# A hybrid encoder trunk in split fp32: the mixer's output projection as seven half-size products, and four MLP blocks begun with half the tokens

## The chip, the cores and the metric

The kernel runs on one core of one Trainium2 chip. The metric is the device time of one execution in microseconds (us), lower is better. The kernel before was run three times: 1082.97, 1083.27 and 1083.28 us, median 1083.27 us. The engines are named as in the profile: PE is TensorE, DVE VectorE, ACT ScalarE, POOL GpSimd, SP the queue that issues the transfers.

## The reference

One layer over 512 tokens of width 1024. What matters here is the end of the token mixing and the MLP:

```python
g = sigmoid(gates + b_gate)
g_ssd, g_attn = g[..., :D_MODEL], g[..., D_MODEL:]
mixed = (g_ssd * y_ssd + g_attn * y_attn) @ w_o          # 512x1024 @ 1024x1024
x = x + rmsnorm(mixed, post_mix_norm)
h = rmsnorm(x, pre_mlp_norm)
f = square(relu(h @ w_mlp_in)) @ w_mlp_out               # width 4096
x = x + rmsnorm(f, post_mlp_norm)
```

`y_ssd` is itself a product with `w_ssd_out` (2048 x 1024). Everything ahead of it (input projection, state-space scan, windowed attention) is the same in both kernels.

## The kernel before

**Products.** Every fp32 operand is split into two parts, `hi` (rounded by a cast on ACT) and `lo` (the rest, a subtract on POOL or DVE), and a product is three matmuls, hi x hi, hi x lo and lo x hi, into one PSUM bank (`mm3`, L436; the matmul is at L430, transposes at L434). A matmul multiplies one 128x128 tile against 512 columns, or 256.

**Order.** The program is a list of quanta (`build`, L1633). Each has weight chunks that are loaded (`wr`, three buffers), split into `wh` and `wl` (three buffers) ahead of time, and a function that issues its matmuls. The program written so is then put in order by a planner (`Planner`, `chain`, L529), which simulates it with costs and due times and fixes one static order of instructions for each engine. An engine works strictly in that order: an instruction that waits holds up all behind it. The order of the SP queue, which issues the loads, is fixed in the same way.

**Buffers.** PSUM has eight banks of 128x512: a ring of three called `pp` and a ring of five called `ps` (`bank`, L395). Other tiles of 128x512 come from 83 SBUF slots (`slots.get`, `slots.put`), handed out again first in, first out.

**The stages around the change**, in order:
- `ssd_out` (`ssd_out_quanta`, L1303): eight blocks of 128 output features, all 512 tokens, 16 k-tiles x 3 = 48 matmuls each. The first two blocks do 14 k-tiles first, and their last two k-tiles come later (`rest`), because the last two tiles of `y` wait for an rstd that passes through small DMAs (`yT` L1235, `yl` L1283). After each block `ssd_out_done` (L1287) applies the gates: two DVE operations into the gate's own SBUF slot (L1290, L1291), then a split with scale 0.5 into `mh` and `ml` (L450, L451), features on the partitions.
- `w_o`: 16 tiles of 128x512, loaded by `load_wo`, split by `split_wo`: cast on ACT (L447), subtract on DVE (L448).
- The mixer (`mix_quantum`, L1354): for each of four token tiles, two halves of 512 output columns, 8 k-tiles x 3 = 24 matmuls each, 192 in all. Then Square with a row sum on ACT (L1369), three 128x1 steps on POOL ending in a `pow` (L421 to L425), the norm, the residual `x1`, a second Square and `pow`, and the scaled rows `h2` (L1374 to L1379).
- `flip_h2` (L1390): 16 PE transposes for each half of the tokens put `h2` with features on the partitions, and ACT and DVE split it (L455, L456). The first is placed before the mixer's last token tile, the second after the first of the MLP's halves.
- `up_halves` (L1465): the first SPL = 3 blocks of the first MLP product are begun with tokens 0 to 255 (24 matmuls of 256 columns each) while the rest is normed and flipped, and finished with tokens 256 to 511. Further blocks take all 512 columns (`up_quantum`). After a pair of blocks, `up_done` and `combine` (L1428) make the operands A11, A12, A22 and S1 to S4 of the second product.
- The second MLP product (`folded_quanta`, L1492) is computed in four parts, each as one 2x2 block product with seven half-size products in place of eight: operands A and S from `combine`, weights B11, B21, B22 and T1 to T4, where T1 to T4 are sums of weight tiles made on DVE (L1510 to L1521). A half-size product is 2 token tiles x 4 k-tiles x 3 = 24 matmuls of 512 columns. Its sums are gathered into `acc` (L1598 copy on ACT, L1601 add on DVE). Part 3 takes the order A11, A12, S2, S1, S4, S3, A22.

The small 128x1 steps of the last norm stand at L1617 and L1619, its multiply by the gain at L1623, its residual update at L1629, its `pow` at L1626.

Of the kernel before, what the change touches and what calls it, by code (L numbers as in the profile page):

```python
# [29 lines left out]
LAST_LO = dict(LO, **{n: [LO[n][0], [(0, 512)]] for n in ('T1', 'T2', 'T3', 'T4')})  # L30

# [337 lines left out]
class Trunk:  # L369
# [917 lines left out]
    def ssd_out_done(self, ps, m):  # L1287
        nc = self.nc
        t = self.gate[m]
        nc.vector.scalar_tensor_tensor(t, t, 1.0, ps, op0=ALU.add, op1=ALU.mult)  # L1290
# [3 lines left out]
        self.slots.put(t, self.gate[8 + m])  # L1294
        self.mix.append((hi, lo))
        if m == 7:
            for a in self.ys:
                self.slots.put(*a)
            for k in range(0, 8, 2):
                self.split_wo(1, k)  # L1300
            self.load_x()

    def ssd_out_quanta(self):  # L1303

        w = self.d_w_ssd_out_b
        banks = []

        def most(parts):
            ps = self.bank("pp")
            banks.append(ps)  # L1310
            for k in range(14):
                wh, wl = parts[k // 8]
# [10 lines left out]
        tail = w[0:2, 1, :, 6:8].rearrange("m p k n -> p m (k n)")  # L1323
        return [Quantum([(w[m, 0], 8, 128, "p"), (w[m, 1, :, :6], 6, 128, "p")], most) for m in range(2)] + [
            Quantum([(tail, 2, 256, "p")], rest)] + [
            self.cm(w, m * 128, lambda: self.ys, lambda ps, m=m: self.ssd_out_done(ps, m)) for m in range(2, 8)]

    def load_wo(self, j, k):

        for i in (k, k + 1):  # L1330
            raw = self.wo_raw[j, i] = self.slots.get("or")
            self.nc.sync.dma_start(raw, self.d_w_o[0, i * 128:(i + 1) * 128, j * 512:(j + 1) * 512])

    def split_wo(self, j, k):
        for i in (k, k + 1):
            raw = self.wo_raw.pop((j, i))
            hi, lo = self.slots.get("oh", dtype=F32R), self.slots.get("ol", dtype=F32R)
            self.split(hi, lo, raw)
            self.slots.put(raw)
            self.wo[j, i] = hi, lo  # L1340
# [13 lines left out]
    def mix_quantum(self, t):  # L1354

        nc = self.nc
        tok = slice(t * 128, (t + 1) * 128)

        def run(_):
            ssq, rs = self.tmp("sq", [128, 4], 4), self.tmp("rs", [128, 2], 4)  # L1360
            h2 = [self.slots.get("h2") for _ in range(2)]
            self.h2t.append(h2)
            ps = []
            for j in range(2):
                p = self.bank("pp")
                for k in range(8):
                    hi, lo = self.mix[k]
                    self.mm3(p, (hi[:, tok], lo[:, tok]), self.wo[j, k], k == 0, k == 7)
                nc.scalar.activation(h2[j], p, AF.Square, accum_out=ssq[:, j:j + 1])  # L1369
                ps.append(p)  # L1370
            self.rsqrt_mean(rs[:, 0:1], ssq[:, 0:2], D)
            for j in range(2):
                x1 = self.x1[t][j]
                nc.vector.scalar_tensor_tensor(h2[j], ps[j], rs[:, 0:1], self.g2[j], op0=ALU.mult, op1=ALU.mult)  # L1374
                nc.vector.tensor_tensor(x1, h2[j], x1, op=ALU.add)
                nc.scalar.activation(h2[j], x1, AF.Square, accum_out=ssq[:, 2 + j:3 + j])
            self.rsqrt_mean(rs[:, 1:2], ssq[:, 2:4], D)
            for j in range(2):
                nc.vector.tensor_scalar(h2[j], self.x1[t][j], rs[:, 1:2], None, op0=ALU.mult)  # L1379
                self.x1d[t, j] = self.dp.tile([128, 512], F32, name=f"x1d{t}{j}")  # L1380
                nc.sync.dma_start(self.x1d[t, j], self.x1[t][j])
                self.slots.put(self.x1[t][j])
            if t == 3:
                for a in list(self.wo.values()) + self.mix:
                    self.slots.put(*a)
                self.slots.put(*self.g2)

        return Quantum([], run)

    def flip_h2(self, t2):  # L1390
# [5 lines left out]
        for k in range(0, 8, 2):  # L1396
            ps = self.bank("ps")
# [67 lines left out]
    def up_halves(self, n):  # L1465

        w = self.d_w_mlp_in_b
        chunks = [(w[m, 0], 8, 128, "p") for m in map(self.block, range(n))]
        held, banks = [], []

        def product(m, t2):
            wh, wl = held[m]
            tok = slice(t2 * 256, (t2 + 1) * 256)
            for k in range(8):
                hi, lo = self.h2[k]
                self.mm3(banks[m][:, tok], (wh[:, k], wl[:, k]), (hi[:, tok], lo[:, tok]), k == 0, k == 7)

        def first(parts):
            held.extend(parts)
            for m in range(n):  # L1480
                banks.append(self.bank("pp" if m < 2 else "ps"))
                product(m, 0)

        def second(m):
            def run(_):
                product(m, 1)
                self.up_done(banks[m], m)
            return run
# [3 lines left out]
    def folded_quanta(self, part):  # L1492
# [4 lines left out]
        raw, banks = {}, {}  # L1497

        def load(name, k):
            i, j = int(name[1]) - 1, int(name[2]) - 1  # L1500
            r0 = (8 * part + 4 * i + k) * 128
            raw[name, k] = get("wd")
            nc.sync.dma_start(raw[name, k], self.d_w_mlp_out[0, r0:r0 + 128, j * 512:(j + 1) * 512])
# [22 lines left out]
        def chunk(name, c):  # L1526
# [9 lines left out]
            far = part == 3 and 2 * order.index(weights[name]) + c in FAR  # L1536

            def make():
# [4 lines left out]
                for n, k in enumerate(ks):  # L1543
# [3 lines left out]
                    for e, q in (LAST_LO if part == 3 else LO)[name][n]:  # L1547
# [7 lines left out]
        def product(a, b, bank, first, to):  # L1555
            def run(parts):
                end = first and part == 3 and a == order[-1]
                if first:
                    banks[bank] = [self.bank("pp" if part == 3 and bank == "Z" else "ps") for _ in range(3 if end else 2)]
                for u in range(2):  # L1560
                    tok = slice(u * 128, (u + 1) * 128)
                    for col in [slice(0, 256), slice(256, 512)] if end and u else [slice(0, 512)]:
                        ps = banks[bank][u + (col.start > 0)]
                        for k in range(4):
                            hi, lo = self.f[part, k][a]
                            wh, wl = parts[k // 2][0][k % 2]
                            self.mm3(ps[:, col], (hi[:, tok], lo[:, tok]), (wh[:, col], wl[:, col]),
                                     first and k == 0, k == 3, not first)
                        for t, j in to:
                            self.gather(2 * t + u, j, ps, col)  # L1570
                            if part == 3 and a == [p for p in order if (t, j) in products[p][3]][-1]:
                                if not self.complete:
                                    self.g4 = self.norm_rows("post_mlp_norm")
                                self.down_done(2 * t + u, j, col)
# [10 lines left out]
        order = ('A11', 'A12', 'S2', 'S1', 'S4', 'S3', 'A22') if part == 3 else ("A11", "S2", "S3", "S1", "A22", "S4", "A12")  # L1585
        weights = {b: a for a, (b, *_) in products.items()}
        if part == 3:
            self.at(len(self.quanta) + BACK, self.load_x1)
            for name, lead in (('B11', 4), ('B22', 4), ('B12', 4), ('B21', 3)):
# [43 lines left out]
    def build(self):  # L1633
        self.Q, self.P, self.T, self.bt, self.at_ = {}, {}, {}, {}, []
        self.gate, self.grp, self.yT, self.ys, self.mix, self.wo, self.wo_raw = {}, {}, [], [], [], {}, {}
# [78 lines left out]
```

## Time and profile before

| | us |
|---|---|
| median of three runs | 1083.27 |
| the profiled execution | 1082.52 |
| its span in the trace | 1080.6 |
| busy in it: PE, DVE, ACT, POOL | 1071.3, 744.5, 640.1, 801.5 |

The page gives busy time by engine, tenths of the span in 40 slices, the chain of work that ended last, and the costliest groups. Other views of the same execution give the chain in order of time, the waits of one engine with what ended them, busy time by stretch, and an engine's instructions on a time line, where neighbours of one kind are run together (x7 is seven of them). Times are counted from the span's start. The rows that matter are quoted in the prediction.

### The profile page before, as it was taken

Reading aid. Unit: us, or ns where it says so; the run is one execution under the profiler, and the core shown is the slowest. Engines: PE = TensorE matmul, PEld = TensorE weight load, DVE = VectorE, ACT = ScalarE, POOL = GpSimd, SP = SyncE. Lnnn points to the kernel's source line nnn. Section 1 sums busy time; section 2 is a strip of 40 time slices with the busy share of each in tenths; the row PEclk is TensorE's granted clock in tenths of the full one; section 3 lists DMA queues with packets and bytes.
Section 4 is the critical chain, followed back from the end, with each engine's and each line's share of the span. In section 5 each row is a group of like instructions: output and inputs, shape, how many; then the busy total and the mean of one; then the engine's idle time right before and its main releaser. Section 6 shows DMA issues by size and latency. Waiting matters only on the chain.

```text
span 1080.6 us, 16563 instructions
## 1 busy us (share of the span) xinstructions
PE 1071.3 (99%) x5542; PEld 898.3 (83%) x5542; DVE 744.5 (69%) x1281; ACT 640.1 (59%) x1378; POOL 801.5 (74%) x986
## 2 busy tenths in 40 slices
PE   9999999999999999999999999999999999999997
PEld 7888888888888888888888888889888888888885
DVE  5777787787786878787886952435573574584698
ACT  7766786686686857676768532324554444444552
POOL 5846558468668898989998976511688898898994
PEclk9999999999999999999999999999999999999998
DMA  8333423433444435343554462514321422524222
GB/s 284 118 103 116 117 79 119 126 115 98 125 126 124 140 114 172 102 159 117 149 151 124 157 191 101 192 62 156 108 69 58 156 90 67 157 88 143 82 98 78
DMA packets 61380, 133.19 MB, mean 123 GB/s; under 512 B 9064, under 2 KB 18792, under 8 KB 61296
## 3 DMA queue, kind: packets, MB, share of 16 engines
q1 hardware_dynamic: 61008, 131.76, 38.9%
q8 instruction: 43, 0.70, 0.3%
q10 hardware_dynamic: 288, 0.39, 0.1%
q14 instruction: 41, 0.34, 0.1%
HBM read 127.63 MB, written 4.49 MB: 122 GB/s over the span
## 4 chain that ended last, share of the span: by engine, by line
PE 97%; DVE 1%; DMA 1%; issue 0%; ACT 0%; SPq 0%; POOL 0%; DVEq 0%; POOLq 0%
PE pp L430 70%; PE ps L430 24%; PE ps L434 3%; DMA wr<-in_wv 1%; DVE P L932 0%; SPq L670 0%; DVE wl L600 0%; DVEq L1710 0%; DVE ag L1623 0%; PE pp L434 0%; POOLq L1710 0%; ACT wh L597 0%; ACT x L740 0%; DVE acc L1601 0%; DVE m L1163 0%
## 5 line engine op out<-in xcount | busy, mean ns | idle before, releaser
L509 POOL TENSOR_TENSOR wl<-wr,wh 128x256 fp32r<-128x256 f32 (+1 forms) x500 | 422.1, 873 | 146.2 <-ACT wh L505 139.3
L430 PE MATMUL pp<-h,wh 128*128 128x512 f32 (+1 forms) x1712 | 524.5, 388 | 0.0
L430 PEld LDWEIGHTS pp<-h,wh 128*128 128x128 f32 x1712 | 316.3, 188 | 62.4 <-issue 1.2
L430 PE MATMUL pp<-h,wl 128*128 128x512 f32 (+1 forms) x856 | 332.0, 388 | 0.0
L505 ACT CAST wh<-wr 128x1024 fp32r<-128x1024 f32 x131 | 136.4, 1041 | 132.7 <-PE pp L430 118.3
L430 PEld LDWEIGHTS pp<-h,wl 128*128 128x128 f32 x856 | 160.9, 188 | 32.2 <-issue 0.2
L1549 POOL TENSOR_TENSOR wl<-wd,wh 128x256 fp32r<-128x256 f32 x158 | 130.7, 865 | 12.1 <-ACT wh L1546 12.0
L1546 ACT CAST wh<-wd 128x512 fp32r<-128x512 f32 x82 | 47.3, 618 | 32.5 <-PE ps L430 15.8
L1417 DVE SCALAR_TENSOR_TENSOR pp<-pp,r 128x512 f32<-128x512 f32 (+1 forms) x31 | 17.6, 568 | 67.6 <-ACT r L1414 67.5
L430 PE MATMUL ps<-wl,fh 128*128 128x512 f32 x164 | 64.0, 390 | 0.0
L430 PE MATMUL ps<-wh,fl 128*128 128x512 f32 x164 | 63.9, 390 | 0.0
L430 PE MATMUL ps<-wh,fh 128*128 128x512 f32 x164 | 63.9, 389 | 0.0
L1160 ACT ACTIVATE n<-cb,tables 128x128 f32<-128x128 f32 x128 | 49.3, 391 | 21.1 <-DVE cb L1151 15.8
L994 DVE SCALAR_TENSOR_TENSOR u<-pp,cv,u 128x510 f32<-128x510 f32 (+1 forms) x64 | 47.7, 745 | 7.0 <-ACT u L990 5.8
L1161 ACT ACTIVATE m<-cb,tables 128x128 f32<-128x128 f32 x128 | 48.8, 388 | 3.8 <-DVE cb L1151 3.6
L430 PE MATMUL pp<-yh,wl 128*128 128x512 f32 x128 | 49.8, 390 | 0.0
L430 PE MATMUL pp<-yh,wh 128*128 128x512 f32 x128 | 49.7, 389 | 0.0
L430 PE MATMUL pp<-yl,wh 128*128 128x512 f32 x128 | 49.7, 389 | 0.0
L1156 ACT ACTIVATE rf<-rf,tables 128x128 f32<-128x128 f32 x128 | 42.5, 392 | 6.1 <-DMA rf<-csT 6.1
L926 ACT ACTIVATE P<-P,mx 128x384 f32<-128x384 f32 (+1 forms) x64 | 35.2, 553 | 15.5 <-DVE mx L923 15.3
L1196 POOL TENSOR_TENSOR w<-w,E 128x256 f32<-128x256 f32 x48 | 38.2, 809 | 7.8 <-DVE w L1192 6.4
L1092 POOL TENSOR_TENSOR xd<-x,tables 128x256 f32<-128x256 f32 x48 | 32.4, 694 | 15.1 <-ACT x L1017 12.8
(273 smaller groups left out, 2162.5 us busy)
## 6 DMA issues: line engine op xcount, KB each, us to landing
wr<-in_w_in_b SPq DMA_DIRECT2D x74, 512.0 KB, 3.6
wr<-in_w_mlp_in_b SPq DMA_DIRECT2D x32, 512.0 KB, 3.5
wd<-in_w_mlp_out SPq DMA_DIRECT2D x64, 256.0 KB, 3.6
rf<-csT SPq DMA_DIRECT2D x32, 256.0 KB, 3.9
rb<-csT SPq DMA_DIRECT2D x32, 256.0 KB, 5.2
wr<-in_w_ssd_out_b SPq DMA_DIRECT2D x14, 512.0 KB, 4.3
x<-in_x SPq DMA_DIRECT2D x16, 256.0 KB, 5.6
E<-csE SPq DMA_DIRECT2D x32, 128.0 KB, 4.7
```

The source lines that it names most:

```text
L430: self.nc.tensor.matmul(out, lhsT, rhs, start=start, stop=stop, skip_group_check=more)
L434: self.nc.tensor.transpose(out, src, self.ident[:n, :n])
L505: self.nc.scalar.copy(hi[:, :m], raw)
L509: engines[e].tensor_tensor(lo[:, c], raw[:, c], hi[:, c].bitcast(F32), op=ALU.subtract)
L926: nc.scalar.activation(p[:, :w], p[:, :w], AF.Exp, bias=mx[:, n:n + 1], accum_out=sm[:, n:n + 1])
L994: nc.vector.scalar_tensor_tensor(u[:, a:e], ps[:, a + d:e + d], self.wtap(t, b), u[:, a:e], op0=ALU.mult, op1=ALU.add)
L1156: nc.scalar.activation(v4(rf)[:, h], v4(rf)[:, h], AF.Identity, bias=ncs[:, 0, h:h + 1])
L1160: nc.scalar.activation(v4(n)[:, h], cb[:, 0], AF.Copy, scale=dt[:, 0, h:h + 1])
L1161: nc.scalar.activation(v4(m)[:, h], cb[:, 1], AF.Copy, scale=dt[:, 1, h:h + 1])
L1196: nc.gpsimd.tensor_tensor(wc, wc, E[:, d], op=ALU.add)
L1546: nc.scalar.copy(hi, src)
L1549: (nc.vector if q == 512 else nc.gpsimd).tensor_tensor(lo[:, c], src[:, c], hi[:, c].bitcast(F32), op=ALU.subtract)
```

## The change

- The mixer's product becomes `folded_quanta("o")`: the same seven products as the MLP's, in the order A11, A12, S2, S1, S4, S3, A22, 168 matmuls. `mixed` gathers them and norms each token tile as soon as both its halves are there: tokens 0 to 255 are complete after S4, the right half of the others after S3, the left half after A22. A22 adds onto a bank that S3 used, after `acc` has taken S3's sum out of it. `load_wo`, `split_wo` and `mix_quantum` go.
- `ssd_out_done` leaves the gated sum in its `pp` bank, and a pair of blocks goes through `combine`, as in the MLP. The blocks come in the order 0, 4, 1, 5, 2, 6, 3, 7. The factor 0.5 is dropped, and the eps of the norm that follows is 4 EPS in its place.
- All lo parts of the `w_o` operands are made on DVE, in single pieces of 512 (`MIX_LO`); `MIX_FAR` says which operands lie in slots of their own, `MIX_LEAD` how early the loads are placed.
- Of the norm's small steps only the `pow` stays on POOL; the others go to DVE.
- The lo parts of the first two `ssd_out` blocks' weights are subtracted on POOL in four pieces each (`YLO`), before in one.
- Four MLP blocks are begun with 256 tokens, before three; the fourth's weights lie in slots (`th`, `tl`), and three of the four banks are `pp`. The first flip takes `pp` banks.
- In `folded_quanta` a branch for a product that begins a bank and is the last in part 3 goes; no product of the kernel before took it.

In the order that results, PE has 5099 instructions before and after (24 matmuls of 512 columns fewer, and 24 more become 48 of 256), DVE 1283 and 1365, ACT 1290 and 1321, POOL 991 and 996, SP 446 and 446.

```diff
+MIX_ORDER = (0, 4, 1, 5, 2, 6, 3, 7)
+MIX_LO = {n: [[(0, 512)], [(0, 512)]] for n in LO}
+YLO = ["pppp"] * 8
+MIX_FAR = (2,3,5,6,8,9,11,12)
+MIX_LEAD = (('B11', 4), ('B21', 3), ('B22', 2), ('B12', 2))
+PP_BANKS = {("o", "Z"), (3, "Z")}
+HALVES, HALF_PP, FLIP1, HALF_LO = 4, 3, 1, "pppp"
...
-    def ssd_out_done(self, ps, m):
-        t = self.gate[m]
-        nc.vector.scalar_tensor_tensor(t, t, 1.0, ps, op0=ALU.add, op1=ALU.mult)
-        nc.vector.tensor_tensor(t, t, self.gate[8 + m], op=ALU.add)
-        hi, lo = self.slots.get("mh", dtype=F32R), self.slots.get("ml", dtype=F32R)
-        self.split(hi, lo, t, 0.5)
...
+    def ssd_out_done(self, ps, n):
+        m = MIX_ORDER[n]
+        t, o = self.gate[m], self.gate[8 + m]
+        nc.vector.scalar_tensor_tensor(ps, t, 1.0, ps, op0=ALU.add, op1=ALU.mult)
+        parts = [(ps, slice(0, 512))] if n % 2 else [(ps, slice(0, 256)), (t, slice(256, 512))]
+        for dst, tok in parts:
+            nc.vector.tensor_tensor(dst[:, tok], ps[:, tok], o[:, tok], op=ALU.add)
+        self.pair.extend(dst[:, tok] for dst, tok in parts)
+        self.slots.put(o)
+        if n % 2 == 0:
+            self.pair.append(t)
+            return
+        self.slots.put(t)
+        self.combine("o", n // 2)
...
-    def mix_quantum(self, t):
...
+    def mixed(self, t, j, ps, col):
+        final = t > 1 and j == 0
+        if not final and (t, j) not in self.acc:
+            self.acc[t, j] = get("acc")
+            nc.scalar.copy(self.acc[t, j], ps)
+            return
+        src = ps
+        if not final:
+            src = self.acc.pop((t, j))
+            nc.vector.tensor_tensor(src, src, ps, op=ALU.add)
...
+        nc.scalar.activation(h2, src, AF.Square, accum_out=ssq[:, seen:seen + 1])
+        nc.vector.tensor_tensor(h2, src, self.g2[j], op=ALU.mult)
+        tail = lambda a, eps: nc.vector.tensor_scalar(rs[:, a:a + 1], ssq[:, a:a + 1], 1.0 / D, eps, op0=ALU.mult, op1=ALU.add)
+        more = lambda a: (nc.vector.scalar_tensor_tensor(rs[:, a + 1:a + 2], ssq[:, a + 1:a + 2], 1.0 / D, rs[:, a:a + 1],
+                                                        op0=ALU.mult, op1=ALU.add),
+                          nc.gpsimd.tensor_tensor(rs[:, a + 1:a + 2], rs[:, a + 1:a + 2], self.mhalf, op=ALU.pow))
+        if seen == 0:
+            tail(0, 4 * EPS)
+            return
+        more(0)
+        for i in range(2):
+            nc.vector.scalar_tensor_tensor(x1[i], h2[i], rs[:, 1:2], x1[i], op0=ALU.mult, op1=ALU.add)
+            nc.scalar.activation(h2[i], x1[i], AF.Square, accum_out=ssq[:, 2 + i:3 + i])
+            if i == 0:
+                tail(2, EPS)
+        more(2)
+        for i in range(2):
+            nc.vector.tensor_scalar(h2[i], x1[i], rs[:, 3:4], None, op0=ALU.mult)
...
 def flip_h2(self, t2):
-            ps = self.bank("ps")
+            ps = self.bank(("pp", "ps")[t2])
...
 def up_halves(self, n):
+        def chunk(n, m):
+            if n < SPL:
+                return (w[m, 0], 8, 128, HALF_LO)
...
+                tiles = [(self.slots.get("th", dtype=F32R), self.slots.get("tl", dtype=F32R)) for _ in range(2)]
+                for i, (hi, lo) in enumerate(tiles):
+                    src = raw[0][:, i * 512:(i + 1) * 512]
+                    self.nc.scalar.copy(hi, src)
+                    for c in (slice(0, 256), slice(256, 512)):
+                        self.nc.gpsimd.tensor_tensor(lo[:, c], src[:, c], hi[:, c].bitcast(F32), op=ALU.subtract)
...
-                banks.append(self.bank("pp" if m < 2 else "ps"))
+                banks.append(self.bank("pp" if m < HALF_PP else "ps"))
...
 def folded_quanta(self, part):
+            w, k0 = (self.d_w_o, 0) if part == "o" else (self.d_w_mlp_out, 8 * part)
...
+            far = 2 * order.index(weights[name]) + c in {"o": MIX_FAR, 3: FAR}.get(part, ())
...
+                    for e, q in {"o": MIX_LO, 3: LAST_LO}.get(part, LO)[name][n]:
...
+                        if part == "o":
+                            self.mixed(2 * t + u, j, ps, col)
+                            continue
...
 def build(self):
-        for i in range(4):
-            self.at(c0 + 1 + i, lambda i=i: self.load_wo(0, 2 * i))
-            self.at(c0 + 2 + i, lambda i=i: self.split_wo(0, 2 * i))
-            self.at(c0 + 6, lambda i=i: self.load_wo(1, 2 * i))
-        self.add(*[self.mix_quantum(t) for t in range(NT)])
+        self.add(*self.folded_quanta("o"))
         self.at(n() - 1, lambda: self.flip_h2(0))
-        self.at(n() + 1, lambda: self.flip_h2(1))
-        self.add(*self.up_halves(SPL))
-        self.add(*[self.up_quantum(i) for i in range(SPL, 8)])
+        self.at(n() + FLIP1, lambda: self.flip_h2(1))
+        self.add(*self.up_halves(HALVES))
+        self.add(*[self.up_quantum(i) for i in range(HALVES, 8)])
```

More of the change, by code (lines that the diff above doesn't have):

```diff
@@ L1352, in load_x1 @@
             self.nc.sync.dma_start(self.x1[t][j], kept)
-    def mix_quantum(self, t):
+    def mixed(self, t, j, ps, col):
         nc = self.nc
[L1357 to L1388, printed above, removed]
@@ new lines, in mixed @@
+        get, put = self.slots.get, self.slots.put
+        final = t > 1 and j == 0
[7 more added lines that the diff above has]
+            nc.vector.tensor_tensor(src, src, ps, op=ALU.add)
+        if not self.h2t:
+            self.ms = self.tmp("mss", [128, 16], 1), self.tmp("mrs", [128, 16], 1)
+            self.h2t = [[None, None] for _ in range(NT)]
@@ L1390, in flip_h2 @@
+        if t == 3:
+            put(*self.g2)
     def flip_h2(self, t2):
@@ L1475, in product @@
                 hi, lo = self.h2[k]
-                self.mm3(banks[m][:, tok], (wh[:, k], wl[:, k]), (hi[:, tok], lo[:, tok]), k == 0, k == 7)
+                self.mm3(banks[m][:, tok], weights(m, k), (hi[:, tok], lo[:, tok]), k == 0, k == 7)
         def first(parts):
@@ L1487, in run @@
                 self.up_done(banks[m], m)
+                if len(chunks[m]) == 3:
+                    for a in held[m]:
+                        self.slots.put(*a)
             return run
@@ L1556, in run @@
             def run(parts):
-                end = first and part == 3 and a == order[-1]
                 if first:
-                    banks[bank] = [self.bank("pp" if part == 3 and bank == "Z" else "ps") for _ in range(3 if end else 2)]
+                    banks[bank] = [self.bank("pp" if (part, bank) in PP_BANKS else "ps") for _ in range(2)]
+                col = slice(0, 512)
                 for u in range(2):
[L1561 to L1574, printed above, removed]
+                    tok, ps = slice(u * 128, (u + 1) * 128), banks[bank][u]
+                    for k in range(4):
+                        hi, lo = self.f[part, k][a]
+                        self.mm3(ps, (hi[:, tok], lo[:, tok]), parts[k // 2][0][k % 2], first and k == 0, k == 3, not first)
+                    for t, j in to:
+                        if part == "o":
+                            self.mixed(2 * t + u, j, ps, col)
+                            continue
+                        self.gather(2 * t + u, j, ps, col)
+                        if part == 3 and a == [p for p in order if (t, j) in products[p][3]][-1]:
+                            if not self.complete:
+                                self.g4 = self.norm_rows("post_mlp_norm")
+                            self.down_done(2 * t + u, j, col)
                 for f in self.held[part]:
@@ L1584, in folded_quanta @@
                     "A12": ("B21", "Z", True, [(0, 0)])}
-        order = ('A11', 'A12', 'S2', 'S1', 'S4', 'S3', 'A22') if part == 3 else ("A11", "S2", "S3", "S1", "A22", "S4", "A12")
+        order = ('A11', 'A12', 'S2', 'S1', 'S4', 'S3', 'A22') if last else ("A11", "S2", "S3", "S1", "A22", "S4", "A12")
         weights = {b: a for a, (b, *_) in products.items()}
-        if part == 3:
-            self.at(len(self.quanta) + BACK, self.load_x1)
-            for name, lead in (('B11', 4), ('B22', 4), ('B12', 4), ('B21', 3)):
+        if last:
+            if part == 3:
+                self.at(len(self.quanta) + BACK, self.load_x1)
+            for name, lead in MIX_LEAD if part == "o" else (('B11', 4), ('B22', 4), ('B12', 4), ('B21', 3)):
                 for k in range(4):
```

58 lines of the change are left out of this document (32 added, 26 removed).

## The prediction

> **What bounds the kernel now.** I read the page first, then TensorE's waits, then the chain of waits around the mixer.
>
> ```profile
> span 1080.6 us, 16563 instructions
> PE 1071.3 (99%) x5542; PEld 898.3 (83%) x5542; DVE 744.5 (69%) x1281; ACT 640.1 (59%) x1378; POOL 801.5 (74%) x986
> DVE  5777787787786878787886952435573574584698
> ```
> ```profile
> PE pp L430 <- DVE two L655: 1.0, 1, 1.0
> ```
>
> TensorE is busy 1071.3 of 1080.6 us, and the longest entry among its waits for other engines is 1.0 us, once. So a matmul that is taken out is worth its whole issue time, until another engine is late. The chain of waits (start, length, what) gives the issue time:
>
> ```profile
> 612.25 118.59 PE pp L430 x523
> ...
> 746.50 2.88 PE pp L430 x24
> ...
> 762.75 27.23 PE pp L430 x120
> ```
>
> 523 matmuls of 512 columns in 118.59 us are 226.7 ns each, so a group of 24 takes 5.44 us. The 24 of 256 columns at 746.50 took 2.88 us, 120 ns each. The second halves of the MLP's first blocks end at 762.75. Around the mixer the other engines have room. Columns: stretch, TensorE busy, its weight loads, DVE, ACT, POOL, clock, DMA share, GB/s:
>
> ```profile
> 680.00:700.00 20.00, 20.00 (x90) 16.59 (x89) 8.25 (x9) 6.60 (x9) 10.07 (x9) 1.00 0.57 190
> 700.00:720.00 20.00, 20.00 (x90) 16.56 (x89) 6.90 (x9) 4.23 (x13) 3.77 (x7) 1.00 0.28 101
> 720.00:740.00 20.00, 20.00 (x98) 16.77 (x97) 9.56 (x19) 8.55 (x24) 3.70 (x12) 1.00 0.18 63
> 780.00:800.00 20.00, 20.00 (x90) 16.56 (x89) 18.48 (x31) 11.08 (x22) 15.46 (x18) 1.00 0.25 86
> ```
>
> The clock is 1.00 throughout, so nothing is gained or lost by it.
>
> **Matmuls.** The mixer's 8 x 24 = 192 matmuls become 7 x 24 = 168, of the same 512 columns: 24 x 226.7 ns = 5.44 us less. The fourth MLP block moves to halves: 24 of 512 columns become 48 of 256, 48 x 120 - 24 x 226.7 ns = +0.32 us. The 32 transposes stay. On TensorE alone: -5.12 us. It holds only while every operand is in time, and the change gives DVE 82 more instructions, so the rest of the sum is a walk along the queues. It uses these durations (mean ns behind the bar):
>
> ```profile
> L448 DVE TENSOR_TENSOR ol<-or,oh 128x512 fp32r<-128x512 f32 x16 | 19.2, 1243 | 0.9 <-ACT oh L447 0.7
> L1601 DVE TENSOR_TENSOR acc<-acc,ps 128x512 f32<-128x512 f32 x28 | 19.1, 682 | 12.5 <-PE ps L430 12.5
> L448 DVE TENSOR_TENSOR fl<-fs,fh 128x512 fp32r<-128x512 f32 x13 | 13.5, 1040 | 1.8 <-ACT fh L447 1.8
> L448 DVE TENSOR_TENSOR fl<-pp,fh 128x256 fp32r<-128x256 f32 x27 | 11.3, 417 | 4.0 <-ACT fh L447 4.0
> L1623 DVE TENSOR_TENSOR ag<-acc,post_mlp_norm 128x512 f32<-128x512 f32 x8 | 6.3, 810 | 0.0
> L1629 DVE SCALAR_TENSOR_TENSOR x<-ag,frs,x 128x512 f32<-128x512 f32 x8 | 5.9, 746 | 0.4 <-POOL frs L1626 0.4
> L1619 DVE SCALAR_TENSOR_TENSOR frs<-fsq,frs 128x1 f32<-128x1 f32 x4 | 1.1, 270 | 0.0
> L1617 DVE TENSOR_SCALAR frs<-fsq 128x1 f32<-128x1 f32 x4 | 0.6, 144 | 0.0
> ```
> ```profile
> L1376 ACT ACTIVATE h<-x 128x512 f32<-128x512 f32 x8 | 5.0, 626 | 10.5 <-DVE x L1375 10.5
> L1376 ACT ACTIVATION_READ_ACCUMULATOR h<-x 128x1 f32 x8 | 1.5, 185 | 0.0
> L509 POOL TENSOR_TENSOR wl<-wr,wh 128x256 fp32r<-128x256 f32 x172 | 142.3, 858 | 53.9 <-ACT wh L505 49.0 <-issue 3.4 <-DMA wd<-in_w_mlp_out 1.4
> L425 POOL TENSOR_TENSOR rs<-rs,mhalf 128x1 f32<-128x1 f32 x8 | 4.3, 543 | 0.7
> ```
>
> **Price of a DVE operation between SBUF tiles.** The change adds many of them, and the mean of such a row mixes two cases, which the timelines of DVE and POOL show apart (start, length):
>
> ```profile
> 631.65 1.96 DVE L1283 TENSOR_TENSOR yl<-yT,yh 128x512 fp32r<-128x512 f32 x2 [0.47 <-ACT yh L1282]
> ...
> 638.36 0.68 DVE L1290 SCALAR_TENSOR_TENSOR gate<-gate,pp 128x512 f32<-128x512 f32 x1
> ...
> 688.86 2.72 DVE L448 TENSOR_TENSOR ol<-or,oh 128x512 fp32r<-128x512 f32 x1
> ...
> 698.23 0.69 DVE L1290 SCALAR_TENSOR_TENSOR gate<-gate,pp 128x512 f32<-128x512 f32 x1 [4.73 <-PE pp L430]
> ...
> 702.49 1.29 DVE L448 TENSOR_TENSOR ol<-or,oh 128x512 fp32r<-128x512 f32 x2
> ```
> ```profile
> 682.94 2.82 POOL L509 TENSOR_TENSOR wl<-wr,wh 128x256 fp32r<-128x256 f32 x4 [1.47 <-ACT wh L505]
> 688.39 2.64 POOL L509 TENSOR_TENSOR wl<-wr,wh 128x1024 fp32r<-128x1024 f32 x1 [2.62 <-ACT wh L505]
> ...
> 699.26 2.64 POOL L509 TENSOR_TENSOR wl<-wr,wh 128x1024 fp32r<-128x1024 f32 x1 [3.04 <-ACT wh L505]
> ```
>
> With POOL idle an `ol` takes 0.645 us (1.29 for two at 702.49). The one at 688.86 took 2.72 us, and POOL's subtract stood beside it from 688.39 to 691.03: it ended 0.55 us after that. So the price is set by whether POOL works at that moment: 0.645 alone, 1.04 to 1.24 beside it. [...]
>
> **Gates and operands (end of `ssd_out`).** The mixer begins when the last block's sum is done, at 698.2; blocks of 48 matmuls are 10.88 us apart, so the seventh ends at 687.35 and the third at 698.23 - 5 x 10.88 = 643.8. The first pair's sums now stay in two of the three `pp` banks until `combine` has read them. The second of the pair is done at about 638.4; two gate operations of 0.69 us and about seven reads of 0.417 us, all with an operand in PSUM, let go of block 0's bank at about 638.4 + 1.4 + 2.9 = 642.7, where no cast on ACT holds them up. The fourth block wants it when TensorE is through with the third, some 0.3 us before that sum is seen done: 643.5, 0.75 us to spare. Later pairs have a whole block, 10.88 us, for the same chain. The `yl` of the last two tiles now come 0.8 to 1 us later, since one small DMA of the rstd chain stands behind a weight load in SP's queue; they end at 633.6 now (the row of 631.65) and are wanted from about 635.5. Cost 0 for both; bounds 0 to 0.75 us each.
>
> From the seventh block's end, 687.35, to 698.2 DVE has 14 two-SBUF operations of 512 (14 x 0.645 = 9.0 us) besides the gate's own (about 1.7 us): 10.7 of 10.85 us, if POOL is idle. It is: the three 1024-wide subtracts of MLP weights that stood at 688.39 to 699.26 come later in the new order, and 682.94's four pieces end at 685.8. From 698.2 DVE has 30 more, until T4's last lo part at about 722, each product's operands 5 to 8 us ahead of TensorE (A11 at 698.2, A12 703.6, S2 709.1, S1 714.5, S4 720.0, S3 725.4, A22 730.84 at 5.44 us each). w_o's 28 lo parts, the T sums and the two norm multiplies are all in this count. ACT has 28 casts more of the size of its Square, 0.626 us, in the same 40 us, against 4.23 to 8.55 busy of 20: hidden.
>
> **The one wait I expect.** A22's first matmul adds into the bank that S3's left half used, which DVE must first have read into `acc`. That read stands behind the norm of the first 256 tokens. From S4's end at 725.4: one `acc` add 0.68, two `x` updates 1.49, one 128x1 step 0.27, one norm multiply 0.81, one 128x1 step 0.14, two `x` updates 1.49, 0.41 for two 128x1 steps, then the `acc` add itself 0.68: 5.97 us, ready at 731.4, against 730.84. The means are taken beside a POOL that works in part, and the two at 702.49 took 0.645 each, not 0.69: some 0.05 us off each of eight, 0.4 in all; POOL's `pow` stands behind four weight pieces of 0.705 to 0.858 (from about 722.5 to 725.3 or 725.9) and a Square of 0.81, which can add 0.3. I take 0.4 us; bounds 0 and 1.1. The cover here is thin: anything later in that chain is paid in full. The second bank is wanted 2.72 us later and is ready at about 734.2 against 734.0: inside the same bound.
>
> **After the mixer.** Tokens 0 to 255 are flipped while A22 runs, so four halves of 2.88 us follow, then the second flip at about 750 with 2 to 3 us to spare, then the second halves. The fourth block's weights use other slots and end before 745. The first `up` block afterwards waits for a bank let go near 762.1, wanted near 763.5. Costed at nothing; without that cover each would be 0 to 1 us. End of the second halves: 762.75 + 5.44 (the fourth block, before done whole after it) = 768.19 now, about 763.5 then. From there both kernels issue the same list.
>
> **Sum.** -5.44 + 0.32 + 0.4 = -4.7 us. The profiled execution took 1082.52 us (span 1080.6 and 1.9 around it): 1077.8. It lies 0.75 us under the median of the runs, 1083.27, so the median forecast is 1078.6 us. With the bounds (stalls of 0 to 2.6 together): 1078.2 to 1080.7.
>
> **Rivals.**
> A. *The norm chain is longer.* The chain into A22 holds five two-SBUF operations (a norm multiply, four `x` updates). If POOL's pieces (2.82 us for four) hold DVE as at 688.86, it is late by up to 2.8 us more: 1080 to 1081.4. For it: the thin cover. Against: the pieces are over by about 725.9, when that chain begins.
> B. *DVE becomes the bound: slower.* Place: the 44 two-SBUF operations from 687 to 722. If they run at 1.04 us, as the `fl` row beside a busy POOL, that is 44 x 0.395 = 17.4 us more; T4 is ready at 739.5, 8.7 us after 730.84: 1078.6 + 8.7 = 1087.3. It takes the whole gain from 13.4 us of backlog, or 0.95 us for each. For it: `ol`'s mean of 1.243 and 14 operations in a slot of 10.85 us. Against: POOL 3.77 and 3.70 us busy of 20 there.
> C. *Banks.* If the first pair's chain takes x us longer than I count, TensorE stands x - 0.75; 5.5 us would eat the gain: 1079 to 1083. [...] Against: later pairs have 10.88 us, so it could happen once.
> D. *Given back in the MLP.* At 780 to 800 DVE is busy 18.48 of 20 us, and TensorE now gets there 4.7 us earlier with the same DVE work behind it. If DVE can't follow, 2 to 4.7 us come back: 1080.6 to 1083.3. Against: TensorE is at 20.00 in that very stretch, and DVE's tenths fall to 5 to 7 after it.
> E. *It doesn't do what it says:* no matmul is saved where it counts, 1083. The order of the changed program has the 24 fewer; nothing speaks for it.
>
> **How the numbers follow.** Forecast 0.62, A 0.14, B 0.10, C 0.04, D 0.08, E 0.02. The likeliest gives 1078.6. A measurement of this kernel can tell 0.2% from no change, 2.2 us, so faster means under 1081.1: the forecast, A almost whole, half of C, a third of D: 0.81. Within: the rest of A, C and D, and E, about 0.07. Slower: B and a little for a larger stall than any named: 0.12. The range starts at 1077.4 (no stall, and the 0.8 us that the walk may err) and goes to 1082.2, through A and half of D; B is left out. The likeliest's own range is 1077.4 to 1080.7.
>
> **What would show it.** Right: the second halves' end near 763.5 in the chain; TensorE's waits grown by one row on DVE's `acc` add, 0 to 1.1 us; w_o's lo parts on DVE near 0.645 us from 687 to 722; 168 mixer matmuls at 226.7 ns. Wrong: a wait of TensorE over 2 us on an operand (B) or a `pp` bank (C), DVE operations at 1 us in the mixer, new waits after 763 (D).

## The result and the profile after

The changed kernel takes 1078.75 us (median of five runs, 1078.30 to 1079.04), before 1083.27 us (five runs, 1082.97 to 1083.72). The ratio is 0.9958, 95% interval 0.9943 to 0.9972: 4.5 us or 0.4% faster, against a forecast of 1078.6 us. The profiled run took 1078.30 us, where the prediction's sum gives 1077.8.

The page of the changed kernel, two of the rows that the prediction shows of the one before:

```profile
span 1076.5 us, 16682 instructions
PE 1066.9 (99%) x5542; PEld 895.6 (83%) x5542; DVE 761.2 (71%) x1363; ACT 655.5 (61%) x1409; POOL 798.3 (74%) x991
```

TensorE has 4.4 us less to do and is still busy for 99% of the span; DVE has 16.7 us more and ACT 15.4. The spans start with a different few tenths of waiting each (first loads and the like), so stretches are compared. `ssd_out` takes 384 x 226.7 ns = 87.08 us in both. The mixer starts at 730.84 - 144 x 226.7 ns = 698.2 before, so `ssd_out`'s first matmul starts at 698.2 - 87.08 = 611.1, and at 611.35 after (the chain's row below). The chains of both end in one group of 108 matmuls, the last products of part 3:

```profile
1045.85 24.49 PE ps L430 x108
```
```profile
611.35 87.08 PE pp L438 x384
698.43 5.44 PE ps L438 x24
703.87 5.44 PE pp L438 x24
709.31 13.61 PE ps L438 x60
...
730.52 0.61 DVE acc L1364
731.12 0.04 issue
731.17 3.02 PE ps L438 x12
734.19 1.31 PE pp L442 x12
...
740.83 8.75 PE pp L438 x72
...
750.30 1.75 PE ps L442 x16
752.05 8.86 PE pp L438 x72
760.91 2.88 PE ps L438 x24
763.79 21.79 PE pp L438 x96
...
1041.48 24.49 PE ps L438 x108
```

(First fence before, second after: start, length, what.) From the first `ssd_out` matmul to the start of the last group it is 434.7 us before and 430.13 after: 4.6 us less, and all of it lies between 698.4 and 763.8. The mixer's start to the end of the second halves, with the fourth block counted in both, took 768.19 - 698.2 = 70.0 us before and 763.79 - 698.43 = 65.36 after. From there to the last group it is 277.7 us in both. So nothing was given back in the MLP.

Three rows of DVE's and one of POOL's time line after (start, length, in brackets the idle time ahead) show how close the mixer runs to DVE's limit, with the stretch 700 to 720:

```profile
693.75 1.29 DVE L1590 TENSOR_TENSOR wl<-wd,wh 128x512 fp32r<-128x512 f32 x2
...
721.37 0.69 DVE L1590 TENSOR_TENSOR wl<-wd,wh 128x512 fp32r<-128x512 f32 x1 [0.22 <-ACT wh L1587]
...
724.51 1.27 DVE L1372 TENSOR_TENSOR h<-acc,post_mix_norm 128x512 f32<-128x512 f32 x1
```
```profile
722.41 2.82 POOL L517 TENSOR_TENSOR wl<-wr,wh 128x256 fp32r<-128x256 f32 x4 [36.39 <-ACT wh L513]
```
```profile
700.00:720.00 20.00, 20.00 (x90) 16.58 (x89) 19.70 (x38) 12.70 (x26) 0.00 (x0) 1.00 0.22 67
```

POOL stands still from 686.0 to 722.4, DVE is busy 19.70 of the 20 us from 700 to 720 at 0.645 us for each lo part (1.29 for two), and TensorE 20.00. As soon as POOL works again a norm multiply with two SBUF inputs takes 1.27 us (0.69 at 713.36, where POOL is idle), and ends at 725.78, 0.55 us after POOL's last piece at 725.23. That hold, rival A's, cost next to nothing here: the matmuls of the sum that DVE adds next ended only at 725.63.

### The profile page after: what moved, and what is told of

Its sections match the earlier page's. It is cut to its first block, busy times and chain, and to the rows that moved or that the text cites. A ratio compares the mean times of both kernels' runs of the same rounds, so it can differ in the third digit from the quotient of the medians.

```text
span 1076.5 us, 16682 instructions
## 1 busy us (share of the span) xinstructions
PE 1066.9 (99%) x5542; PEld 895.6 (83%) x5542; DVE 761.2 (71%) x1363; ACT 655.5 (61%) x1409; POOL 798.3 (74%) x991
## 4 chain that ended last, share of the span: by engine, by line
PE 96%; DVE 1%; DMA 1%; issue 0%; ACT 0%; POOL 0%; SPq 0%; POOLq 0%; DVEq 0%
PE pp L438 66%; PE ps L438 27%; PE ps L442 3%; DMA wr<-in_wv 1%; PE pp L442 0%; DVE P L940 0%; DVE x L1385 0%; DVE acc L1364 0%; SPq L678 0%; DVE wl L608 0%; DVE ag L1664 0%; DVE h L1372 0%; POOLq L1747 0%; ACT wh L605 0%; POOL mrs L1378 0%
## 5 line engine op out<-in xcount | busy, mean ns | idle before, releaser
L517 POOL TENSOR_TENSOR wl<-wr,wh 128x256 fp32r<-128x256 f32 (+1 forms) x517 | 417.3, 837 | 179.8 <-ACT wh L513 176.4
L1587 ACT CAST wh<-wd 128x512 fp32r<-128x512 f32 x92 | 53.2, 618 | 38.4 <-PE pp L438 19.8
L438 PE MATMUL ps<-wl,fh 128*128 128x512 f32 x184 | 71.8, 390 | 0.0
L438 PE MATMUL ps<-wh,fl 128*128 128x512 f32 x184 | 71.7, 390 | 0.0
L438 PE MATMUL ps<-wh,fh 128*128 128x512 f32 x184 | 71.7, 390 | 0.0
L1425 DVE SCALAR_TENSOR_TENSOR pp<-pp,r 128x256 f32<-128x256 f32 (+1 forms) x31 | 17.3, 559 | 66.1 <-ACT r L1422 65.9
```

Of the source, the lines that this page charges most:

```text
L438: self.nc.tensor.matmul(out, lhsT, rhs, start=start, stop=stop, skip_group_check=more)
L517: engines[e].tensor_tensor(lo[:, c], raw[:, c], hi[:, c].bitcast(F32), op=ALU.subtract)
L1587: nc.scalar.copy(hi, src)
```

## The experiments

Each is the changed kernel with one edit. Times are medians of 4 to 10 runs; where a run is set against the changed kernel, 1078.75 us and its stretch of 430.13 us (first `ssd_out` matmul to the last group) are meant. The kernel before, run beside all of them, had medians of 1083.09 to 1083.23 us.

**1. Half of product A12 left out** (12 of 24 matmuls).

```diff
-                    for k in range(4):
+                    ks = range(2, 4) if (part, a) == ("o", "A12") else range(4)
+                    for k in ks:
...
```

> Left out: half of product A12 (its first two k-tiles, 12 of 24 matmuls). The theory that only TensorE's own time bounds the stage, with operands 5 to 8 us ahead, expects 12 x 226.7 ns = 2.7 us off the changed kernel's 1078.75: 1076.0. The rival, that the seven-product stage is by now just as much bound by DVE (19.70 of 20 us busy from 700 to 720 in the changed kernel, the last lo part of T4 done at 722.06, just ahead of the add that opens the norm chain at 722.95), expects that the chain can begin only some 0.9 us sooner while A22 is wanted 2.7 us sooner: a new wait of about 1.8 us ahead of A22 and 1077.9.

Measured 1080.42 us: slower by 1.7, though TensorE has 2.7 us less to do. Its longest wait, three rows of 1 us behind it (columns as in the prediction), and two rows of the chain ahead of it:

```profile
PE ps L438 <- DVE acc L1364: 3.3, 1, 3.3
```
```profile
732.00:733.00 1.00, 1.00 (x5) 0.81 (x4) 0.93 (x2) 0.83 (x3) 1.00 (x2) 0.77 1.05 397
733.00:734.00 1.00, 1.00 (x3) 0.72 (x3) 1.00 (x2) 0.00 (x0) 0.93 (x2) 0.50 1.06 410
...
735.00:736.00 1.00, 1.00 (x7) 1.00 (x6) 0.20 (x1) 0.04 (x1) 0.65 (x1) 0.52 0.53 213
```
```profile
726.80 1.06 ACT wh L513
727.86 2.46 ACT h L1386 x8
```

Both theories missed. S4's first sum was added at 720.01, 2.9 us sooner than in the changed kernel, so DVE's operands were not what held it; no product waited for one. But the read that A22 waits for stands behind the four `x` updates, and behind 128x1 steps that need their Squares, in both kernels. (Here DVE stood idle 0.36, 0.46 and 0.36 us for Squares between 728.8 and 730.35, though S3's last matmul was over at 728.1: what waits holds up what stands behind it.) The planner orders anew for every kernel, and here it put a weight cast of the MLP on ACT ahead of all four Squares: the cast begins at 726.80, the Squares end at 730.32, and the read stood at 730.60, as late as in the changed kernel (730.43). TensorE waited 3.3 us, and then came something nobody had priced: its clock was 0.50 from 732.5 to 736.0. 2.7 us less work, 3.2 more waiting and 1.75 lost to the clock are +2.2; the stretch is 432.14, +2.0.

**2. Product A12 done twice** (24 matmuls more).

```diff
+                    ks = list(range(4)) * (2 if (part, a) == ("o", "A12") else 1)
+                    for n, k in enumerate(ks):
...
```

> Product A12 is done twice (24 matmuls more, its sum is doubled). If every matmul of this stage is paid at its issue time, +24 x 226.7 ns = 5.4 us, less the 0.1 us that A22 waits now: 1084.1, and A22 waits for nothing. If the stage is set by the other engines, TensorE has room and it is less: 1079 to 1082.

1084.1 us, the stretch 435.48, +5.35. A product of 24 matmuls is worth its issue time here, which is the term of 5.44. The expectation that A22 then waits for nothing was wrong: S3 ends at 698.54 + 7 x 5.44 = 736.62, and A22 starts at 736.70. The chain ahead of A22 starts with S4's sum and moves with TensorE, so the small wait stays whatever room DVE has ahead of it.

**3. S3 before S4** in the mixer's order, so that tokens 0 to 255 end one product later.

```diff
-        order = ('A11', 'A12', 'S2', 'S1', 'S4', 'S3', 'A22') if last else ...
+        order = ('A11', 'A12', 'S2', 'S1', 'S3', 'S4', 'A22') if part == "o" else ...
```

> S3 goes before S4, so the first 256 tokens end one product later (5.44 us) and A22's bank is free early. The theory that the early end of these tokens is what covers their norm and flip expects: A22's wait gone (-0.1 us), the scaled rows ready near 739 in place of 734, the flip no longer inside A22 and TensorE standing 2 to 3 us behind A22's end at 736.5: 1080.7 to 1081.7. The rival, that the gain is in the count of matmuls alone and the order is free, expects 1078.7.

1085.63 us: slower than the kernel before (ratio 1.0022, 1.0013 to 1.0032), with the same 5.1 us of matmuls saved. Its longest wait, and what DVE and POOL did ahead of it:

```profile
PE pp L442 <- DVE h L1391: 4.5, 2, 4.3
```
```profile
731.92 2.43 DVE L1385 SCALAR_TENSOR_TENSOR x<-h,mrs,x 128x512 f32<-128x512 f32 x2
...
740.45 3.18 DVE L1391 TENSOR_SCALAR h<-x,mrs 128x512 f32<-128x512 f32 x4 [1.20 <-POOL mrs L1378]
```

The direction was as expected, the size was not. The scaled rows start at 740.45 in place of 731.10, since pairs of `x` updates take 2.4 us beside POOL's weight pieces, 1.4 before, and POOL's `pow` stands behind such pieces. TensorE waits 4.5 us, and its clock is 0.50 from 740.3, still in the wait, to 747.1. Ending the first tokens one product later cost 6.9 us in this order of the planner's: more than the whole product that the change saves.

**4. The lo parts of `w_o` on POOL** in pieces of 256 columns.

```diff
-MIX_LO = {n: [[(0, 512)], [(0, 512)]] for n in LO}
+MIX_LO = LO
```

> The lo parts of w_o's operands go from DVE (28 of 512 columns) to POOL (56 of 256), which has no work from 686 to 722. If DVE and POOL only have to share the count of work, DVE gets 28 x 0.61 = 17 us free and POOL needs 56 x 0.705 = 39.5 us for a gap of 36 us: about 0 to 4 us slower, 1079 to 1083. If an operation of DVE with two SBUF inputs and POOL's subtract exclude each other, the sums T, the norm and the remaining splits on DVE rise from 0.61-0.69 to about 1.0 to 1.3 us each, POOL's pieces from 0.705 to 0.86 and more, operands come late one after the other and it is 5 to 15 us slower: 1084 to 1094.

1088.74 us (ratio 1.0051, 1.0034 to 1.0068). DVE's operations between SBUF tiles from 687 to 723, this kernel first, then the changed one:

```profile
L1562 DVE TENSOR_TENSOR wd<-wd,wd 128x512 f32<-128x512 f32 x4 | 4.3, 1070 | 0.6 <-POOL tl L1590 0.6
L1552 DVE TENSOR_TENSOR wd<-wd,wd 128x512 f32<-128x512 f32 x4 | 4.0, 990 | 0.6 <-POOL wl L1590 0.6
```
```profile
L1562 DVE TENSOR_TENSOR wd<-wd,wd 128x512 f32<-128x512 f32 x4 | 2.6, 690 | 0.0
L1552 DVE TENSOR_TENSOR wd<-wd,wd 128x512 f32<-128x512 f32 x4 | 2.6, 690 | 0.0
```

The same sums take 0.99 to 1.07 us beside POOL and 0.69 without it. POOL's pieces average 0.74 to 1.09 us by group. The last of them, for A22's weights, ends at 740.1; POOL's `pow` stands among them, the scaled rows come late, and TensorE waits 6.7 us for these ahead of the flip, with its clock at 0.50 from 735.0 to 745.2.

**5. The gated sums in SBUF** as before the change.

```diff
-        nc.vector.scalar_tensor_tensor(ps, t, 1.0, ps, op0=ALU.add, op1=ALU.mult)
+        nc.vector.scalar_tensor_tensor(t, t, 1.0, ps, op0=ALU.add, op1=ALU.mult)
+        nc.vector.tensor_tensor(t, t, o, op=ALU.add)
...
```

> The gated sums of ssd_out go into the gate's own SBUF slots as before the change, all else as in the changed kernel. The theory that the place of the sums earns nothing by itself (TensorE does not wait in this stage either way) expects 1078.75 within 0.5 us, no TensorE wait on a pp bank, and combine's DVE operations longer only where POOL works (640 to 686). The rival, that sums left in PSUM carry part of the gain because they keep DVE off the SBUF side, expects late operands for the first products and 1080 to 1083.

1078.81 us, the stretch 430.15: no difference. `combine`'s splits from SBUF take longer, and its reads are hidden:

```profile
L456 DVE TENSOR_TENSOR fl<-gate,fh 128x256 fp32r<-128x256 f32 x8 | 6.6, 823 | 0.0
```

0.823 us each on average, against 0.42 from PSUM. Leaving the sums in PSUM saves DVE time that nothing waited for.

**6. Three blocks begun with 256 tokens**, as before.

```diff
-HALVES, HALF_PP, FLIP1, HALF_LO = 4, 3, 1, "pppp"
+HALVES, HALF_PP, FLIP1, HALF_LO = 3, 3, 1, "pppp"
```

> Three MLP blocks begun with 256 tokens in place of four. By matmul time alone -0.32 us (1078.4). The scaled rows of the last 256 tokens are ready at 748.0 now and the second flip stands at 750.3; without the fourth half it is wanted at about 747.4. If the fourth half is the cover of that norm, TensorE waits 0.5 to 2 us there: 1079 to 1080.5. If the cover was never needed: 1078.4.

1082.08 us, slower by 3.3 and beyond the expectation. The 16 transposes of the second flip took 2.30 us in place of 1.75, but the long wait stands elsewhere:

```profile
PE pp L438 <- DVE ft L1455: 2.0, 1, 2.0
```
```profile
761.00:762.00 1.00, 1.00 (x5) 0.80 (x4) 1.00 (x2) 0.37 (x1) 1.00 (x2) 0.76 0.38 57
762.00:763.00 1.00, 1.00 (x4) 0.72 (x3) 1.00 (x3) 0.00 (x0) 1.00 (x2) 0.50 0.72 229
...
764.00:765.00 1.00, 1.00 (x3) 0.78 (x3) 0.00 (x0) 0.00 (x0) 0.58 (x1) 0.54 0.00 0
```

The first whole block after the halves wants a `pp` bank that `combine` still reads. With a fourth half TensorE has 5.76 us of other work meanwhile. So that half covers the release of a bank more than the norm, and the expectation had the wrong place. (All three halves lay in `pp` banks here; the kernel before had the third in a `ps` bank, which was not tried.) 2.0 of wait, 0.55 in the flip and 1.7 of half clock less 0.32 are 3.9; the stretch is 434.00, +3.9.

**7. The first two `ssd_out` blocks' lo parts in one POOL operation each.**

```diff
-YLO = ["pppp"] * 8
+YLO = ["p"] * 2 + ["pppp"] * 6
```

> The lo parts of the first two ssd_out blocks' weights are again single POOL operations of 1024 and 768 columns. If long POOL operations hold DVE's two-SBUF operations for their whole length, the last two tiles of yl (ready at 635.0 now) come up to 2.6 us later and TensorE waits 0 to 2 us near 636: 1078.7 to 1080.7. If the four pieces only spread the same work, nothing changes: 1078.75.

1078.76 us. The last `yl` ends at 637.1 in place of 635.0, and TensorE does not wait for it: there was more room than the prediction counted (635.5). The delay is of the size that was expected for a hold of DVE, but it is not one: DVE's two `yl` operations took 1.46 us, 2.37 in the changed kernel. The rstd itself came later in this kernel's order: its copy on ACT began at 613.02 in place of 611.52, its `pow` on POOL at 623.58 in place of 621.89, and its last DMA was issued at 629.51 in place of 626.36.

**8. The halves' lo parts in one POOL operation each.**

```diff
-HALVES, HALF_PP, FLIP1, HALF_LO = 4, 3, 1, "pppp"
+HALVES, HALF_PP, FLIP1, HALF_LO = 4, 3, 1, "p"
```

> The lo parts of the weights for the halves are single POOL operations of 1024 columns in place of four of 256. In the changed kernel the norm multiply at 724.51 takes 1.27 us, 0.59 more than its neighbours, and ends 0.55 us after POOL's last piece at 725.23. If a POOL operation holds the multiply for its whole length, one long piece (2.64 us from 722.4, to 725.05) holds it about as long as the last of four does: A22's wait stays within 0 to 0.5 us of the 0.1 us now, and later in the norm of the last tokens a hold of up to 2.6 us shows in a residual update: 1078.7 to 1080.5. If there is no such hold, DVE's operations stay at 0.68 and 1078.75.

1079.18 us, a wait of 0.3 us ahead of the first flip, A22's wait as it was. The hold did not show in a residual update, but plainly in the four scaled rows. This kernel first, with POOL beside it, then the changed one:

```profile
731.24 4.51 DVE L1391 TENSOR_SCALAR h<-x,mrs 128x512 f32<-128x512 f32 x4
732.20 2.40 POOL L517 TENSOR_TENSOR wl<-wr,wh 128x1024 fp32r<-128x1024 f32 x1
```
```profile
731.10 2.86 DVE L1391 TENSOR_SCALAR h<-x,mrs 128x512 f32<-128x512 f32 x4
732.06 3.18 POOL L517 TENSOR_TENSOR wl<-wr,wh 128x256 fp32r<-128x256 f32 x4
```

The third of the four rows begins with POOL's operation: it takes 2.69 us from 732.19 here, and ends at 734.88, 0.28 us after POOL. In the changed kernel it takes 1.03 us from 732.05 and ends 0.29 us after POOL's first piece. The four rows of the last tokens, at 746.20 there, took 1.83 us in all.

**9 to 12. One, two, three and four more reads of the bank that A22 waits for**, to make the wait longer step by step.

```diff
             nc.vector.tensor_tensor(src, src, ps, op=ALU.add)
+            if (t, j) == (2, 1):
+                junk = get("junk")
+                for _ in range(1):   # 1, 2, 3, 4
+                    nc.vector.tensor_tensor(junk, src, ps, op=ALU.mult)
+                put(junk)
```

> One more DVE operation (0.68 us) reads the bank that A22 waits for; its result is not used. If a wait of TensorE is paid once and no more, the wait ahead of A22 grows from 0.1 to 0.1-0.7 us and the time is 1078.75 to 1079.4, the clock 1.00 all through. If any wait lowers the granted clock, some 1.7 us more: 1080.5 to 1081.1.

> Two more DVE operations read that bank. A wait of 0.7 to 1.4 us. Paid once: 1079.4 to 1080.0. Runs with waits of 2.0 and 3.3 us showed a clock of 0.50 for about 3.4 us after them; if that begins with waits this short as well, 1.7 us more: 1081.1 to 1081.7.

> Three more DVE operations read that bank. A wait of 1.2 to 2.0 us. Paid once: 1079.9 to 1080.7. With a half clock of 3.4 us after it: 1081.6 to 1082.4.

> Four more DVE operations read that bank. A wait of 1.8 to 2.7 us, as long as the one of 2.0 us that was followed by a half clock for 3.4 us. Paid once: 1080.5 to 1081.4. With the half clock: 1082.2 to 1083.1.

| reads added | median us | waits of TensorE ahead of the flip, us | half clock in the trace | stretch, against 430.13 |
|---|---|---|---|---|
| 1 | 1081.80 | 0.6 + 0.8 | none | +1.8 |
| 2 | 1082.43 | 0.6 + 1.0 | 733.4 to 736.8 | +3.3 |
| 3 | 1083.10 | 0.6 + 1.1 + 0.7 | 734.8 to 738.2 | +4.0 |
| 4 | 1083.88 | 0.9 + 0.9 + 0.7 | 737.5 to 744.3 | +5.5 |

All four medians lie above what was expected, and the edit did not do quite what it was meant to. The planner put the added reads behind or between the four scaled rows and moved the flip ahead of A22, so TensorE waits for the scaled rows and no longer for the bank, and the first step is larger than one read: 3.05 us. Of these the trace's stretch holds 1.8; the rest was not taken apart. Each further read adds 0.63 to 0.78, about a read's 0.68. The medians take in executions with and without the half clock and the differences outside the stretch, so the traces, not the steps, show the clock's part. In the trace of the second kernel the rows of 1 us behind the waits show the clock (0.68, 0.50, 0.50, 0.62):

```profile
733.00:734.00 1.00, 0.79 (x4) 0.79 (x5) 1.00 (x3) 0.67 (x2) 1.00 (x2) 0.68 0.92 344
734.00:735.00 1.00, 1.00 (x7) 0.81 (x5) 1.00 (x3) 0.77 (x2) 1.00 (x2) 0.50 0.19 72
735.00:736.00 1.00, 1.00 (x6) 0.84 (x5) 1.00 (x3) 0.75 (x3) 1.00 (x2) 0.50 0.00 0
736.00:737.00 1.00, 1.00 (x4) 0.86 (x4) 1.00 (x3) 0.42 (x2) 1.00 (x3) 0.62 0.54 74
```

1.6 us of waiting less the 0.1 of the changed kernel, and 1.7 of half clock, are 3.2 of the +3.3. With one read, 1.3 us in two pieces, the profiled run kept 1.00. In the fourth kernel's trace 2.5 less 0.1 and 3.4 of half clock are 5.8 for the +5.5; a part of that half clock falls into the last wait. (Its profiled run, 1087.28 us, was the slowest of its ten for another wait early in the program, outside the stretch.)

## Why the prediction was right

- **Matmuls, -5.44 + 0.32.** Right; experiment 2 prices a product at 5.35 us.
- **The wait ahead of A22, 0.4 us (0 to 1.1).** The right place and the right chain. From S4's end at 725.63 to the end of the read at 731.11 the chain took 5.48 us, where 5.97 less 0.4 and 0.3 more were counted (5.87), and S3 ends at 698.43 + 6 x 5.44 = 731.07. By the modelled ends in the chain A22 starts 0.1 us late. The starts on TensorE's time line show more (last matmul of S3, first two of A22):

```profile
730.68 0.39 PE L438 MATMUL ps<-th,fl 128*128 128x512 f32 x1
731.17 0.50 PE L438 MATMUL ps<-th,fc 128*128 128x512 f32 x1
731.50 0.39 PE L438 MATMUL ps<-tl,fc 128*128 128x512 f32 x1
```

  Against 0.227 us from start to start the first step loses 0.26 and the second 0.11. Small pauses follow behind the flips, and groups of 72 half-width matmuls take 8.75 and 8.86 us in place of 8.64. From A22's start, 24 x 226.7 ns, two flips of 1.75 and eight groups of 2.88 would end at 763.15; it was 763.79. With the 0.1 these are 0.74 us, where the kernel before lost 0.25 in the same way (730.84 + 31.66 = 762.50, it was 762.75). So the sum is -5.12 + 0.5 = -4.6, forecast -4.7. The term was of the right size, in part by luck: the chain was 0.4 us shorter than counted, and the time that TensorE loses in starting again, which no term held, made up for it.
- **From the profiled run to the median.** The 0.15 us between the forecast, 1078.6, and the median is luck as well. The profiled run was forecast at 1077.8 and took 1078.30, and it lies 0.45 us under its median, not 0.75 as before. The two errors cancel in part.
- **Gates, `yl`, banks at 0.** Right: 384 matmuls in 87.08 us in both. Block 0's bank came free near 643.2, not 642.7, with no wait; `yl` came 1.4 us later by the span's clock (1.2 from `ssd_out`'s start), not 0.8 to 1, and experiment 7 delayed it by 2.1 more at no cost.
- **DVE between 687 and 722.** Right nearly to the operation: 14 operations until 698.2, the last lo part of the mixer's weights at 722.06 (forecast 722). One behind the other they start 0.60 us apart, a little closer than the 0.645 that was counted. It rests on POOL's idleness, as said: experiment 4 put POOL to work there, which is rival B's condition: 1.04 us was forecast for an operation, 0.99 to 1.07 measured; 1087.3 us forecast, 1088.74 measured. The road was not all rival B's: the lo parts that came late were POOL's own (740.1), and TensorE waited for the scaled rows rather than for them.
- **The second flip and the banks behind it.** The flip stood at 750.30 (forecast 750). The bank that was named there (let go near 762.1, wanted near 763.5) was let go at 762.3 and used from 763.79; it is what experiment 6 ran into.
- **Rivals C and D.** No new wait on a `pp` bank came up, and the 277.7 us behind the second halves are the same in both kernels.
- **What the prediction left out** does not show in its time: the clock stayed at 1.00 here, but rivals A, C and D priced a wait at its length. In the traces of experiments 1, 3, 6, 10, 11 and 12 waits of 1.6 us or more cost some 1.5 to 3 us on top. By these numbers a chain late by 2 us would have cost up to 3.7 and left about 1 us of the gain (an estimate); the step from fully hidden to lost can be steeper than the rivals' range said.

Not tried apart: the slots and the lead of the loads (`MIX_FAR`, `MIX_LEAD`), and the norm's small steps on DVE. Every experiment's kernel was also put in order anew by the planner, so each shows its edit together with that order.

## What to carry to other kernels

Where one engine is busy for 99% of the time, work that is taken off it is worth its issue time (24 matmuls 5.35 us in experiment 2) as long as no wait takes its place, and the order that ends part of the rows early (6.9 us here) can be worth more than the product saved (5.4). Before work is put on DVE, look whether POOL is idle in that stretch: the same operation cost 0.69 us without POOL's pieces and 0.99 to 1.07 beside them (experiment 4). And do not price a wait of TensorE at its length alone: from 1.6 us on, every trace here shows some 1.5 us or more on top, though not every run of a kernel seems to pay it.

## What the runs showed of the hardware that was not expected

Seven traces show a lower clock of TensorE behind or within a short wait. The granted clock fell to 0.50 for 3.4 us at waits of 3.3 us (experiment 1), 2.0 (6), 1.6 in two pieces (10) and 2.3 in three (11), for 6.8 us at 4.3 (3, from 740.3 to 747.1) and 2.5 in three pieces (12), and for 10.2 us at 6.7 (4): once, twice or three times 3.4. Matmuls of 512 columns then start 0.427 us apart in place of 0.227. The clock stayed at 1.00 behind waits of 0.1 and 0.3 us, behind the one of 1.0 at the start of the span (traces of before and after), and, in the run profiled, behind 1.3 us in two pieces (9). The fall came after the wait, 1.4 us after the end of the one at 758.1 to 760.1 in experiment 6, or within it (at 740.3 in the one that ends at 741.0 in experiment 3, at 735.0 in the one that ends at 738.7 in 4).

Nor does it seem to come in every run. Of experiment 6's ten runs, the four fastest (1079.96 to 1081.19 us) have a mean clock of 0.998 or 0.999, the other six (1081.78 to 1085.29) 0.996 or 0.997; 3.4 us at half clock are 0.0016 of a span. The mean is a rough sign: the clock also falls to 0.50 behind the last matmul, 3.4 us after its end in the changed kernel's trace (at 1072.1) and 2.0 us after it in that of the kernel before (at 1075.0), so kernels without a half clock before that show 0.998 or 0.997 too. And in experiments 10 and 11 the runs with 0.998 are no faster than those with 0.996 (medians 1082.5 and 1082.6 us, 1083.0 and 1082.7). So the price on top of a wait is shown by the traces, stretch by stretch, and by experiment 6's runs, not by the runs of every kernel. What starts the half clock and what sets its length is not shown.

A DVE operation with one SBUF tensor was held as well: the third scaled row of experiment 8 (`TENSOR_SCALAR`) took 2.69 us beside one POOL operation of 2.40 us, and 0.49 where POOL was idle (747.15 in the changed kernel).
